# Weight-stationary blocks as three products of 256 columns into half a bank

## The chip, the core and the metric

The kernel runs on one core of a Trainium2 chip. The time is device microseconds (us) of one execution; lower is better. TensorE (PE) multiplies and has a second row in the profile for its weight loads (PEld); VectorE (DVE), ScalarE (ACT) and GpSimd (POOL) do the rest; SyncE (SP) issues the weight transfers. PSUM has eight banks of 512 fp32 columns on 128 partitions; the kernel uses four as accumulators (`acc`) and four for everything else (`aux`).

## The reference

One decoder block for 256 tokens and a model width of 2048, all in fp32:

```
a = rmsnorm(x) ; proj = a @ w_in            # 17408 columns
q_a, k_a, v_a, q_r, f_r, i_r, g_r, gate_a, gate_r = split(proj)
q, k = rotary(q_a), rotary(k_a)              # 3 groups x 8 heads of 128
A = windowed attention in 3 groups, mixed by their softmax denominators
R = gated linear recurrence (q_r, f_r, i_r), normed per head, times silu(g_r)
y = sigmoid(gate_a) * (A @ w_attn_branch) + sigmoid(gate_r) * (R @ w_hgrn_branch)
h = x + rmsnorm(y @ w_mix_out)
h = h + rmsnorm((silu(g) * u) @ w_ffn_down)  # g, u = rmsnorm(h) @ w_ffn_gate_up
```

## The kernel before

Every large product is made of fp32r matmuls. Each operand is split into a high part (rounded to fp32r by ACT, line L242 for weights) and a low part (the remainder, DVE, L243), and a product is high x high + high x low + low x high. The activations lie transposed in `xT` (`Split`): per `k` (128 of the 2048 inner rows) a slot holds the high part of 256 tokens and right behind it the low part, so the two can be read as 512 columns in a row; the third value that a call of `Split` returns, `both`, is that.

The work is a list of blocks, each cut into chunks of 512 KB of weights, and one loop runs over all chunks. In each turn it splits the weights of the chunk two ahead (ACT, then DVE), issues the load of the chunk eight ahead (SP), multiplies the present chunk, and then advances by one step each the oldest evacuation (`evacs`) and two lanes of side work (the two recurrences and the attention heads). Each is a Python generator, so what it issues stands in the engines' queues at that place. Engines take their queues in order. Waits come from the tiles' dependencies. There are two kinds of block:

- "N": activations stationary, weights moving. A block is 512 output columns; token half `s` has a bank of its own. Per `k` and half three matmuls of 512 columns. In the V blocks (`parity`) the stationary slice takes every second token.
- "W": weights stationary, activations moving, so that the result comes out transposed (heads on partitions). A block is 256 output columns, two heads, `s` = 0 and 1; 16 `k` in four chunks of four. There are 32 W blocks: for `f_r` and `q_r` (2 x 2 each) and for rotary `q` and `k` (24).

In a W block before, each head has a bank. Per `k` and head two matmuls: the high weights by `both` (512 columns, so the left half of the bank collects high x high and the right half high x low), and the low weights by the high activations (256 columns, added into the left half). The order of the two alternates with `k`. When the block is done, `both_halves` makes the sum: ACT copies the right halves to a tile `sum` (L200), DVE adds the left halves (L202), and the evacuation proper (`evac_f`, `evac_qr` or `evac_rope`) works from `sum` in SBUF. `evac_rope` does nothing in its first step, in its second multiplies the swapped halves by the sine table (L677, two operations on 64 partitions), and in its third multiplies `src` in place by the cosine table (L683) and adds the two into `qk` in an order with even tokens first (L684).

All matmuls pass through the helper at L115, the weight loads of W and N blocks alike. The recurrences' small products stand in PE's queue between the chunks; they wait for DVE's product L776, which follows the masked copy L787; POOL works for them at L770 and L777.

Of the kernel before, what the change touches and what calls it, by code (L numbers as in the profile page):

```python
# [16 lines left out]
AF = mybir.ActivationFunctionType  # L17
OP = mybir.AluOpType

P = 128  # L20
S = 256
# [56 lines left out]
def tile_hybrid_block(ctx: ExitStack, tc: tile.TileContext, t, out):  # L78
    nc = tc.nc
# [25 lines left out]
    def acc_bank():  # L105
        return accp.tile([P, 512], F32, tag="acc", name=nm("acc"))
# [7 lines left out]
    def mm(ps, lhsT, rhs, start, stop):  # L114
        nc.tensor.matmul(ps, lhsT, rhs, start=start, stop=stop, skip_group_check=True)  # L115
# [51 lines left out]
    def ptile(s):  # L167
        pool, n = (act_pool[0], 2) if act_pool else (fp, 5)
        return pool.tile([P, 512], F32, tag="p", bufs=n, name=nm(s))
# [16 lines left out]
    def add(*args, **kw):  # L186
        b = Block(*args, **kw)
        blocks.append(b)
        for c in range(b.steps):
            chunks.append([b, c, None, None, None])  # L190

    def add_wide(w, nk, col, xs, ev):
        for i in range(2):
            add("W", w, nk, col + 256 * i, xs, both_halves(ev, i))

    def both_halves(ev, i):
        def go(banks):
            s = ptile("sum").rearrange("p (h t) -> p h t", h=2)
            for n, ps in enumerate(banks):
                nc.scalar.activation(s[:, n, :], ps[:, S:], AF.Copy)  # L200
            for n, ps in enumerate(banks):
                nc.vector.tensor_add(s[:, n, :], ps[:, :S], s[:, n, :])  # L202
            yield from ev(i, s)
        return go

    def parts(j):

# [37 lines left out]
    def multiply(j, sides=(0, 1)):  # L245
        b, c = chunks[j][:2]
        wh, wl = (w.rearrange("p (k c) -> p k c", k=b.per) for w in chunks[j][3:])
        if b.banks is None:
            b.banks = [acc_bank() for _ in range(2)]
        for s in sides:  # L250
            if s == 1 and c == 0 and b.mid:
                b.mid()
            for kk in range(b.per):
                k = b.per * c + kk
                first, last = k == 0, k == b.nk - 1
                xh, xl, both = b.xs(k)
                if b.kind == "N":
                    ps = b.banks[s]
                    if b.parity:
                        sh, sl = (  # L260
                            x.rearrange("p (j two) -> p two j", two=2)[:, s, :]
                            for x in (xh, xl)
                        )
                    else:
                        sh, sl = (x[:, s * P : (s + 1) * P] for x in (xh, xl))
                    mm(ps, sh, wh[:, kk, :], first, False)
                    mm(ps, sh, wl[:, kk, :], False, False)
                    mm(ps, sl, wh[:, kk, :], False, last)
                    continue
                h, l = (w[:, kk, s * P : (s + 1) * P] for w in (wh, wl))  # L270
                pair = [(b.banks[s], h, both), (b.banks[s][:, :S], l, xh)]
                for i, (ps, x, y) in enumerate(pair if k % 2 == 0 else pair[::-1]):
                    mm(ps, x, y, first and i == 0, last and i == 1)

    def add_wide_block(*args, **kw):
        b = Wide(*args, **kw)
# [52 lines left out]
    def multiply_wide(n, sides=(0, 1), groups=(0, 1)):  # L329
        b, i = steps[n][:2]  # L330
        m, by7 = b.order[i]
        parity = wides.index(b) % 2

        def bank(key, side):
            if key not in b.bank:
                b.bank[key] = acc_bank() if (parity == 0) == (side == 1) else aux()
            return b.bank[key]

        def prod(key, x, w, j, last=False):
            ps = bank(key, 0 if type(key) is tuple else 1)  # L340
            wh, wl = (v[:, j * 512 : (j + 1) * 512] for v in w)
            mm(ps, x[0], wh, key not in b.open, False)
            mm(ps, x[0], wl, False, False)
            mm(ps, x[1], wh, False, last)
            b.open.add(key)

        def act_of(s, k):
            return [x[:, s * P : (s + 1) * P] for x in b.xs(2 * m + k)[:2]]

        w = steps[n][3]  # L350
        if not by7:
            for s in sides:
                for g in groups:
                    for k in range(2):
                        prod((s, g), act_of(s, k), w, 2 * g + k, i == len(b.order) - 1 and k == 1)
            return
        t, d, sums = w[:2], w[2:], b.seven(m)
        last = i == b.last7
        prod((0, 1), act_of(0, 1), d, 2)
        prod((0, 0), sums(3), d, 0)  # L360
        prod("p1", act_of(0, 0), d, 1, last)
        prod("p6", sums(1), t, 2, last)
        prod("p5", sums(0), t, 1, last)
        prod("p7", sums(2), t, 0, last)
        prod((1, 1), act_of(1, 1), t, 3)
# [29 lines left out]
    class Split:  # L395
# [6 lines left out]

        def __call__(self, k):
            x = self.slots[k // 2]
            both = self.flat[k // 2][:, k % 2 * 512 : k % 2 * 512 + 512]
            return x[:, k % 2, 0, :], x[:, k % 2, 1, :], both

        def f32(self, k):
            return self(k)[0].bitcast(F32)
# [256 lines left out]
    def evac_rope(key, tab, then=None):  # L666

        cos = tabs[:, tab, :]
        sin = tabs[:, tab + 1, :]

        def ev(i, src):
            if i == 0:
                qkT[key] = fslot("qk").rearrange("p (h t) -> p h t", h=4)
            yield
            w = ptile("w").rearrange("p (h t) -> p h t", h=2)
            for o, n in ((0, 64), (64, 0)):
                nc.vector.tensor_mul(  # L677
                    w[o : o + 64], src[n : n + 64],
                    sin[n : n + 64, None, :].to_broadcast([64, 2, S]),
                )  # L680
            yield
            u = src
            nc.vector.tensor_mul(u, src, by_rows(cos, 2))  # L683
            nc.vector.tensor_add(  # L684
                qkT[key][:, 2 * i : 2 * i + 2, :].rearrange("p h (two j) -> p h two j", two=2),
                u.rearrange("p h (j two) -> p h two j", two=2),
                w.rearrange("p h (j two) -> p h two j", two=2),
            )
            if i == 1 and then:
                then()  # L690
        return ev
# [5 lines left out]
    def attention(half, h):  # L697
        o = None
        for par in range(2):
            own = slice(par * P, (par + 1) * P)  # L700
            ps = aux()
            for g in range(3):
                q, k = qkT["q", half, g], qkT["k", half, g]
                if g == 0:
                    mm(ps[:, :S], q[:, h, own], k[:, h, :], True, True)
                else:
                    mm(ps[:, P * (g + 1) : P * (g + 2)], q[:, h, own], k[:, h, own], True, True)
            yield
            p = ptile("p")
            m = small("m")  # L710
            nc.vector.tensor_tensor_reduce(
                out=p, in0=ps, in1=amask[:, par, :], scale=1.0, scalar=3e38,
                op0=OP.add, op1=OP.min, accum_out=m[:, 0:1],
            )
            nc.scalar.activation(p, p, AF.Exp, scale=-1.0, bias=m[:, 0:1], accum_out=m[:, 1:2])
            yield
            nc.vector.reciprocal(m[:, 2:3], m[:, 1:2])
            nc.vector.tensor_scalar(p, p, m[:, 2:3], None, op0=OP.mult)
            yield
            yield  # L720
            ps = aux()
            for c in range(4):
                cols = slice(c * P, (c + 1) * P)
                nc.tensor.transpose(ps[:, cols], p[:, cols], ident)  # L724
            yield
            pt = ptile("pt")
            nc.scalar.activation(pt, ps, AF.Copy)
            yield
            if o is None:
                o = aux()  # L730
            for c in range(4):
                v = vN[half, max(c - 1, 0)][:, c if c < 2 else par, h * P : (h + 1) * P]
                mm(o[:, own], v, pt[:, c * P : (c + 1) * P], c == 0, c == 3)
            yield
        hi, lo, _ = attnT(4 * half + h)
        ov = o[:, :S].rearrange("p (two j) -> p two j", two=2)
        nc.scalar.activation(hi.rearrange("p (j two) -> p two j", two=2), ov, AF.Copy)
        nc.vector.tensor_sub(
            lo.rearrange("p (j two) -> p two j", two=2), ov,
            attnT.f32(4 * half + h).rearrange("p (j two) -> p two j", two=2),  # L740
        )
        yield
# [697 lines left out]
```

## Time and profile before

| what | value |
|---|---|
| time, median of 3 runs | 1741.58 us (1741.17 to 1743.07) |
| profiled execution | span 1740.1 us from its first to its last instruction (its only time on the page) |
| PE | 1725.0 us busy, 8424 matmuls, as many loads |
| DVE / ACT / POOL | 1264.3 / 886.1 / 74.0 us busy |
| DMA | 325.91 MB, mean 187 GB/s |
| W blocks | from 56 to 652 us of the span, with V, I and N work between |
| matmuls in W blocks | 1024 of 512 columns and 1024 of 256 |
| `sum`: L200 / L202 | 64 operations each, 20.5 us on ACT, 23.9 us on DVE |

A matmul's busy time in such a table runs from its start to a modelled end and overlaps the next one's; the distance from one start to the next is what counts for a stream of them. The groups of instructions name output and inputs as out<-in: `acc<-xT,w` are the W blocks' products, `acc<-w,xT` the N blocks'. A timeline row gives start, length, engine, line and the number of instructions merged into it. The idle time behind the bar of a group, with what ended it, is time in which that engine waited.

### The profile page before, as it was taken

How to read it: one execution, taken by the hardware profiler on the slowest of the kernel's cores; microseconds unless marked ns; L12 is line 12 of the kernel's file. 1: busy time of each engine (PE TensorE's matmuls, PEld its weight loads, DVE VectorE, ACT ScalarE, POOL GpSimd, SP SyncE). 2: the span in 40 equal slices, each digit the busy share in tenths (PEclk: the TensorE clock that was granted, in tenths of full speed). 3: DMA queues.
4: the chain of work that ended last, by engine and by line, in shares of the span. 5: the costliest groups of instructions: out<-in, count | busy, mean ns of one | idle time of the engine just before them, and what ended most of it. 6: DMA issues, size and time to landing. Idle time of an engine off the chain costs nothing.

```text
span 1740.1 us, 21588 instructions
## 1 busy us (share of the span) xinstructions
PE 1725.0 (99%) x8424; PEld 1448.6 (83%) x8424; DVE 1264.3 (73%) x1372; ACT 886.1 (51%) x1050; POOL 74.0 (4%) x54
## 2 busy tenths in 40 slices
PE   9999999999999999999999999999999999999997
PEld 7888888888888888888888877888888888888886
DVE  5767647877546776544566577888888888898998
ACT  6545455344444444454444466555555555665663
POOL 0002413400000000000000000000000000000000
PEclk9999999999999999999999999999999999999999
DMA  7655445455454554455555745655555555666553
GB/s 271 202 192 194 145 150 165 146 160 186 163 170 161 185 188 169 170 169 193 193 179 185 266 168 175 214 199 201 205 194 194 194 194 199 221 209 218 195 197 116
DMA packets 201222, 325.91 MB, mean 187 GB/s; under 512 B 10096, under 2 KB 76832, under 8 KB 201120
## 3 DMA queue, kind: packets, MB, share of 16 engines
q1 hardware_dynamic: 198848, 319.41, 54.4%
q10 hardware_dynamic: 2272, 5.12, 0.8%
q8 instruction: 66, 1.08, 0.2%
q14 instruction: 36, 0.29, 0.1%
HBM read 322.40 MB, written 2.10 MB: 186 GB/s over the span
## 4 chain that ended last, share of the span: by engine, by line
PE 95%; DVE 2%; ACT 1%; issue 1%; DMA 0%; POOL 0%; DVEq 0%; ACTq 0%
PE acc L115 71%; PE aux L115 22%; DVE w L243 1%; ACT w L242 1%; DVE w L677 0%; PE aux L453 0%; PE aux L724 0%; DMA gpost<-in_norm_mix_post 0%; PE acc L1127 0%; DVE fz L1256 0%; PE aux L1127 0%; DVE x L776 0%; PE aux L440 0%; ACT junk L1210 0%; POOL x L770 0%
## 5 line engine op out<-in xcount | busy, mean ns | idle before, releaser
L243 DVE TENSOR_TENSOR w<-raw,w 128x1024 fp32r<-128x1024 f32 (+1 forms) x353 | 444.4, 1260 | 365.5 <-ACT w L242 362.7
L242 ACT ACTIVATE w<-raw 128x1024 fp32r<-128x1024 f32 (+1 forms) x353 | 372.9, 1057 | 481.1 <-PE acc L115 470.7
L115 PE MATMUL acc<-w,xT 128*128 128x512 f32 x1728 | 409.1, 395 | 0.0
L115 PEld LDWEIGHTS acc<-w,xT 128*128 128x128 f32 x1728 | 326.3, 191 | 65.8
L115 PE MATMUL acc<-xT,w 128*128 128x256 f32 (+1 forms) x2048 | 362.6, 338 | 0.0
L115 PEld LDWEIGHTS acc<-xT,w 128*128 128x128 f32 x2048 | 313.0, 189 | 45.1
L308 DVE TENSOR_TENSOR wl<-raw,w 128x2048 fp32r<-128x2048 f32 x82 | 187.5, 2287 | 34.0 <-ACT w L306 33.9
L306 ACT ACTIVATE w<-raw 128x2048 fp32r<-128x2048 f32 x82 | 156.6, 1910 | 81.7 <-PE aux L115 32.1
L115 PE MATMUL acc<-w,hT 128*128 128x512 f32 x622 | 182.5, 392 | 1.5 <-DVE w L243 1.2
L115 PEld LDWEIGHTS acc<-w,hT 128*128 128x128 f32 x622 | 115.8, 188 | 26.9 <-DVE w L243 2.5
L115 PE MATMUL aux<-w,hT 128*128 128x512 f32 x430 | 135.7, 389 | 0.0
L324 DVE TENSOR_TENSOR wl<-sum,w 128x2048 fp32r<-128x2048 f32 x42 | 96.2, 2290 | 33.8 <-ACT w L320 32.7
L317 ACT ACTIVATE w<-sum 128x1024 fp32r<-128x1024 f32 x42 | 44.7, 1063 | 111.0 <-DVE sum L312 106.7
L115 PEld LDWEIGHTS aux<-w,hT 128*128 128x128 f32 x430 | 80.7, 188 | 16.7
L115 PE MATMUL acc<-w,yT 128*128 128x512 f32 x384 | 88.0, 390 | 0.3 <-DVE w L243 0.3
L115 PEld LDWEIGHTS acc<-w,yT 128*128 128x128 f32 x384 | 71.8, 188 | 15.5 <-DVE w L243 0.7
L115 PE MATMUL acc<-w,a 128*128 128x512 f32 x268 | 83.7, 389 | 0.0
L115 PE MATMUL aux<-w,a 128*128 128x512 f32 x268 | 83.7, 389 | 0.0
L115 PE MATMUL aux<-wl,hT 128*128 128x512 f32 x215 | 83.7, 389 | 0.0
L115 PE MATMUL acc<-wl,hT 128*128 128x512 f32 x215 | 83.7, 389 | 0.0
L326 DVE TENSOR_TENSOR dl<-raw,dh 128x1536 fp32r<-128x1536 f32 x42 | 73.5, 1751 | 0.0
L323 ACT ACTIVATE dh<-raw 128x1536 fp32r<-128x1536 f32 x42 | 61.9, 1474 | 0.0
(263 smaller groups left out, 2015.3 us busy)
## 6 DMA issues: line engine op xcount, KB each, us to landing
raw<-in_w_in SPq DMA_DIRECT2D x271, 512.0 KB, 4.5
raw<-in_w_ffn_gate_up SPq DMA_DIRECT2D x176, 512.0 KB, 4.4
raw<-in_w_ffn_down SPq DMA_DIRECT2D x88, 512.0 KB, 4.8
raw<-in_w_mix_out SPq DMA_DIRECT2D x32, 512.0 KB, 4.9
raw<-in_w_attn_branch SPq DMA_DIRECT2D x16, 512.0 KB, 4.5
raw<-in_w_hgrn_branch SPq DMA_DIRECT2D x16, 512.0 KB, 4.6
hx<-in_x ACTq DMA_DIRECT2D x4, 512.0 KB, 9.9
x<-in_x SPq DMA_DIRECT2D x3, 512.0 KB, 10.0
```

Source lines behind the costliest of these rows:

```text
L115: nc.tensor.matmul(ps, lhsT, rhs, start=start, stop=stop, skip_group_check=True)
L242: nc.scalar.activation(wh[:, k], raw[:, k], AF.Copy)
L243: nc.vector.tensor_sub(wl[:, k], raw[:, k], wh[:, k].bitcast(F32))
L306: nc.scalar.activation(hi, raw, AF.Copy)
L308: nc.vector.tensor_sub(lo, raw, hi.bitcast(F32))
L317: nc.scalar.activation(hi[:, :1024], s[:, :1024], AF.Copy)
L323: nc.scalar.activation(dhi, d, AF.Copy)
L324: nc.vector.tensor_sub(lo, s, hi.bitcast(F32))
L326: nc.vector.tensor_sub(dlo, d, dhi.bitcast(F32))
```

## The change

A W block uses one bank: head `s` = 0 the left half, `s` = 1 the right. Per `k` and head there are three matmuls of 256 columns into that half: high weights by high activations, high weights by low activations, low weights by high activations. The high weights are loaded for each of the two. Only the block's very first matmul carries the start flag, since it resets the whole bank. The sum is thus complete in the bank: `both_halves` with its copies and additions is gone, and the evacuations are handed the bank itself. As the bank is not overwritten in place, `evac_rope` now writes the cosine product, already in the even-first order, into `qk` and adds the sine product there. `both` goes away.

```diff
-            add("W", w, nk, col + 256 * i, xs, both_halves(ev, i))
-
-    def both_halves(ev, i):
-        def go(banks):
-            s = ptile("sum").rearrange("p (h t) -> p h t", h=2)
-            for n, ps in enumerate(banks):
-                nc.scalar.activation(s[:, n, :], ps[:, S:], AF.Copy)
-            for n, ps in enumerate(banks):
-                nc.vector.tensor_add(s[:, n, :], ps[:, :S], s[:, n, :])
-            yield from ev(i, s)
-        return go
+            add("W", w, nk, col + 256 * i, xs, both_heads(ev, i))
+
+    def both_heads(ev, i):
+        return lambda banks: ev(i, banks[0].rearrange("p (h t) -> p h t", h=2))
...
-            b.banks = [acc_bank() for _ in range(2)]
+            b.banks = [acc_bank() for _ in range(2 if b.kind == "N" else 1)]
...
-                xh, xl, both = b.xs(k)
+                xh, xl = b.xs(k)
...
                 h, l = (w[:, kk, s * P : (s + 1) * P] for w in (wh, wl))
-                pair = [(b.banks[s], h, both), (b.banks[s][:, :S], l, xh)]
-                for i, (ps, x, y) in enumerate(pair if k % 2 == 0 else pair[::-1]):
-                    mm(ps, x, y, first and i == 0, last and i == 1)
+                ps = b.banks[0][:, s * S : (s + 1) * S]
+                mm(ps, h, xh, first and s == 0, False)
+                mm(ps, h, xl, False, False)
+                mm(ps, l, xh, False, last)
...
-            u = src
-            nc.vector.tensor_mul(u, src, by_rows(cos, 2))
-            nc.vector.tensor_add(
-                qkT[key][:, 2 * i : 2 * i + 2, :].rearrange("p h (two j) -> p h two j", two=2),
-                u.rearrange("p h (j two) -> p h two j", two=2),
-                w.rearrange("p h (j two) -> p h two j", two=2),
-            )
+            d = qkT[key][:, 2 * i : 2 * i + 2, :].rearrange("p h (two j) -> p h two j", two=2)
+            nc.vector.tensor_mul(
+                d,
+                src.rearrange("p h (j two) -> p h two j", two=2),
+                cos.rearrange("p (j two) -> p two j", two=2)[:, None, :, :]
+                .to_broadcast([P, 2, 2, P]),
+            )
+            nc.vector.tensor_add(d, d, w.rearrange("p h (j two) -> p h two j", two=2))
```

More of the change, by code (lines that the diff above doesn't have):

```diff
@@ L347, in act_of @@
         def act_of(s, k):
-            return [x[:, s * P : (s + 1) * P] for x in b.xs(2 * m + k)[:2]]
+            return [x[:, s * P : (s + 1) * P] for x in b.xs(2 * m + k)]
         w = steps[n][3]
@@ L404, in __call__ @@
             x = self.slots[k // 2]
-            both = self.flat[k // 2][:, k % 2 * 512 : k % 2 * 512 + 512]
-            return x[:, k % 2, 0, :], x[:, k % 2, 1, :], both
+            return x[:, k % 2, 0, :], x[:, k % 2, 1, :]
         def f32(self, k):
@@ L734, in attention @@
             yield
-        hi, lo, _ = attnT(4 * half + h)
+        hi, lo = attnT(4 * half + h)
         ov = o[:, :S].rearrange("p (two j) -> p two j", two=2)
```

## The prediction

> **What bounds the kernel now.** I read the page first: totals, chain, groups.
>
> ```profile
> span 1740.1 us, 21588 instructions
> PE 1725.0 (99%) x8424; PEld 1448.6 (83%) x8424; DVE 1264.3 (73%) x1372; ACT 886.1 (51%) x1050; POOL 74.0 (4%) x54
> PE 95%; DVE 2%; ACT 1%; issue 1%; DMA 0%; POOL 0%; DVEq 0%; ACTq 0%
> L115 PE MATMUL acc<-xT,w 128*128 128x512 f32 x1024 | 327.3, 398 | 0.0
> L115 PE MATMUL acc<-xT,w 128*128 128x256 f32 x1024 | 201.8, 278 | 0.0
> ```
>
> TensorE is busy for 99% of the span and carries 95% of the chain. The last two rows (groups with shapes kept apart) are the products that the change touches: 1024 of 512 columns and 1024 of 256, stationary `w`, moving `xT`. I call one of each, the work of one `k` and one side, a pair. There are 1024 pairs. A matmul's duration overlaps the next one's, so the mean of 398 ns is no price; the spacing of starts is. For that I took the chain of waits in a stretch that holds only such blocks, and then the timeline of PE in long even stretches.
>
> ```profile
> 559.91 80.12 PE acc L115 x460
> 545.81 94.45 PE L115 MATMUL acc<-xT,w 128*128 128x512 f32 x541
> 764.62 77.68 PE L115 MATMUL acc<-w,xT 128*128 128x512 f32 x342
> 433.69 6.70 PE L115 MATMUL acc<-w,xT 128*128 128x512 f32 x28
> L115 PE MATMUL acc<-w,xT 128*128 128x512 f32 x355 | 80.6, 389 | 0.0
> L115 PE MATMUL acc<-w,xT 128*128 128x512 f32 x28 | 6.7, 394 | 0.0
> ```
>
> The first row is the whole chain from 560 to 640 us: PE alone. So in these blocks a nanosecond per pair is a nanosecond of the kernel, and all other work is cover. Second row (start, length, count): leaving off the last matmul's 0.40 us (398 ns above), 540 spacings fill 94.05 us, 174.2 ns each, **348.3 ns a pair**. Third row: an "N" block (512-column products only, stationary `xT`): (77.68 - 0.39) / 341 = 226.7 ns. Fourth row: the same in a V block, whose stationary slices take every second element: (6.70 - 0.39) / 27 = 233.6 ns. The 0.39 is the mean duration in the last two rows, the groups of 760 to 840 and of 434 to 440 us.
>
> **The change on PE.** A pair (512 and 256 columns, two weight loads) becomes a triple (three times 256 columns, three weight loads). Columns stay at 768; one matmul with its load is added, 1024 times. The one question is what a matmul costs beyond its columns.
>
> Take a matmul as a + c for 256 columns. The N block says a + 2c = 226.7, the pair 2a + 3c = 348.3; so c = 2 x 226.7 - 348.3 = 105.1 and a = 16.5 ns. That is the upper end: +16.5 ns a triple. For the lower end I need the fastest that 512 columns go past anywhere:
>
> ```profile
> 1022.26 1.47 PE L115 MATMUL aux<-warm 128*128 128x512 bf16 x6
> 1023.57 0.27 PE L453 MATMUL aux<-ident,h 128*128 128x128 f32 x1
> 208.72 1.90 PE L115 MATMUL aux<-ones,x 128*128 128x1 f32 x16
> L115 PE MATMUL aux<-ones,x 128*128 128x1 f32 x32 | 3.8, 249 | 0.0
> ```
>
> Six 512-column matmuls on `warm` occupy 1023.57 - 1022.26 = 1.31 us, 218 ns each, anything fixed included. 768 columns at that rate are 327 ns, so the pair holds at least (348.3 - 327) / 2 = 10.6 ns beyond columns per matmul. Third row: matmuls with one moving column and a fresh 128-column load each come every (1.90 - 0.25) / 15 = 110 ns, so a load alone fills about 110 ns and just fits behind 256 columns.
>
> Why should a hidden load cost anything? The V blocks show it: only the layout of the stationary operand differs, and every 512-column matmul takes 6.9 ns more (233.6 against 226.7), though a load of 110 ns has 226 to hide in. So loading is not free for the stream beside it. I take the middle of 10.6 and 16.5, 13.6 ns: the lower end counts what is fixed in a `warm` matmul as columns, so it is too low, and the upper one holds only if a column of moving `xT` costs what a column of moving `w` does, which no row shows. 1024 x 13.6 ns = **+13.9 us** (bounds +10.9 and +16.9).
>
> The Trainium skill ("TensorE: Matmul & The Clock Gate", part 2, on LDWEIGHTS) says the opposite: PE has two independent read ports, and loading the next weights takes no bandwidth from the running matmul. Its section on the back-to-back issue gap would make the addition about 2.5 ns, an estimate of 1024 x 2.5 ns = 2.6 us. The V blocks' 6.9 ns disagree, so the sum does not go by it.
>
> **The change beside PE.** Rows from the groups with shapes kept apart:
>
> ```profile
> L200 ACT ACTIVATE sum<-acc 128x256 f32<-128x256 f32 x64 | 20.5, 371 | 0.0
> L202 DVE TENSOR_TENSOR sum<-acc,sum 128x256 f32<-128x256 f32 x64 | 23.9, 415 | 0.0
> L677 DVE TENSOR_TENSOR w<-sum,tabs 64x512 f32<-64x512 f32 x48 | 39.4, 820 | 1.1
> L683 DVE TENSOR_TENSOR sum<-sum,tabs 128x512 f32<-128x512 f32 x24 | 16.4, 684 | 0.0
> L684 DVE TENSOR_TENSOR qk<-sum,w 128x512 f32<-128x512 f32 x24 | 16.6, 692 | 1.0
> L1015 DVE TENSOR_TENSOR zg<-acc,gpost 128x512 f32<-128x512 f32 x8 | 5.5, 683 | 4.4 <-DMA gpost<-in_norm_mix_post 4.4
> ```
>
> - Removed: 64 ACT copies (20.5 us) and 64 DVE additions (23.9 us). In the even blocks the chain is PE alone, so this returns nothing there. If they had been on the path it would be 44 us.
> - L677, L683 and the products with `rowb` read the bank instead of `sum`. L1015 reads a bank at 683 ns, L683 reads `sum` at 684: no difference. The stride of two moves from the add into the product as well; L684 already reads both inputs with that stride at 692 ns. At worst 8 ns on 24 operations, hidden.
> - The bank is now held until the product at L683 has read it, in the third step after the block, about three chunks. A chunk is 8 pairs, 2.8 us, so 8.4 us. Against that a block takes one bank of four instead of two, so a bank comes up again four blocks (44 us) later; where a V block follows and takes two, the older block ended 11 us before. Cost nothing; without that cover PE would wait up to 8.4 us at such a place. Waits of DVE on PE do not move ahead: the split of the next chunk stands before the evacuation in DVE's queue, as now.
> - No DMA and nothing in SP's or POOL's queue is moved. Weight chunks are consumed more slowly, so loads and splits get easier.
>
> **Where DVE does stop PE.** Only beside the second recurrence (waits of PE, timelines of POOL and DVE, line L787, L677 from 560 to 640 us, stretches):
>
> ```profile
> PE aux L115 <- DVE x L776: 2.0, 3, 1.5
> 295.32 1.27 POOL L777 TENSOR_TENSOR x<-x,q 128x512 f32<-128x512 f32 x1 [1.91 <-ACT x L774]
> 296.56 2.47 POOL L770 TENSOR_TENSOR x<-b 128x1024 f32<-128x1024 f32 x1
> 295.43 4.15 DVE L677 TENSOR_TENSOR w<-sum,tabs 64x512 f32<-64x512 f32 x2
> 302.07 1.31 DVE L787 COPY_PREDICATED at<-lmask,aux 128x512 f32<-128x512 int32 x1
> L787 DVE COPY_PREDICATED at<-lmask,aux x12: 702/725/1320, 173.7 to 333.8; 128x512 f32<-128x512 int32 x12
> L677 DVE TENSOR_TENSOR w<-sum,tabs 64x512 f32<-64x512 f32 x14 | 9.6, 685 | 0.3
> 303.00:307.00 4.00, 2.55 (x21) 2.35 (x21) 4.00 (x3) 1.60 (x3) 3.32 (x2) 0.99 0.00 0
> 307.00:310.00 3.00, 3.00 (x12) 2.51 (x11) 3.00 (x6) 0.00 (x0) 0.00 (x0) 0.50 0.46 131
> ```
>
> PE loses 2.0 us in three waits on L776, 1.45 of it between 303 and 307 (busy 2.55 of 4.00), and right after it the granted clock is 0.50, 3 us that give back half, 1.5 us. Before that wait two L677 take 4.15 us while POOL works instead of 2 x 0.685. After the change L677 has one operand less in SBUF, and PE comes later by 4% in the same stretch. Both shrink the wait: at most all of it and the slow clock, -3.5 us; at worst another slow stretch, +1.5. I take -2.0. Here a page speaks too: the Trainium skill ("SBUF — State Buffer", who interferes with whom) has only DVE operations with two SBUF inputs contend with POOL's reads, which would take L677 out of it. L787 reads one of its inputs from a bank and still took 1.31 us under POOL against a median of 0.725, so I count on about half.
>
> **Sum.** The executions' median (1741.58) lies 1.5 us over this execution's span; I add to the median: 1741.6 + 13.9 - 2.0 = **1753.5 us**, +0.7%. Its own range: 1741.6 + 10.9 - 3.5 = 1749 to 1741.6 + 16.9 + 1.5 = 1760.
>
> **The rivals.** *Spacings as recorded (faster).* Single starts in an even stretch:
>
> ```profile
> 100.31 0.39 PE L115 MATMUL acc<-xT,w 128*128 128x256 f32 x2
> 100.43 0.51 PE L115 MATMUL acc<-xT,w 128*128 128x256 f32 x2
> 100.54 0.40 PE L115 MATMUL acc<-xT,w 128*128 128x512 f32 x1
> 100.77 0.39 PE L115 MATMUL acc<-xT,w 128*128 128x512 f32 x1
> ```
>
> The starts of a 256-column matmul and its successor lie 0.12 and 0.11 us apart, 0.115 on average, those of a 512-column one 0.23. If 115 ns is what such a matmul costs in any company, the triple takes 345 ns, 3.3 less than the pair: -3.4 us, with -2.0 at DVE's waits 1736 us. It decides if a matmul of 256 columns can keep under 116.1 ns (a third of 348.3) in a row of its own kind. For it: it is the operation itself. Against: it makes the 512-column matmul 233, while N blocks with the same shapes do it in 226.7, and nothing explains that; if instead the short ones run ahead and the long ones pay, the pair comes out by the N blocks' rate. Only sums over a whole period are safe.
>
> *Same columns, same time.* If the pair's 348.3 is a rate per column and loads are hidden, the triple takes 348.3 too: 1741.6 - 2.0 = 1739.6, no change. This is what the skill's two ports would give. Against it stand the V blocks again.
>
> *Loads become the bound (slower still).* 110 ns of load behind 109 of columns leaves no slack. If the load stretches by what it takes from the stream, 110 + 16.5 = 126.5 ns, a triple takes 379.5, +31.2 ns, +31.9 us: 1772 us. Against: two short matmuls in a row show no such spacing now.
>
> **How the numbers follow.** Chances: fixed cost per matmul 0.64 (1753.5), recorded spacings 0.18 (1736), same time 0.11 (1739.6), loads bound 0.07 (1772). 0.2% (3.5 us) is about what a measurement of this kernel can tell from no change. The first and last are slower: 0.71. Recorded spacings are faster: 0.18. Same: 0.11. The range goes from 1736, which takes in the case of no change and the upper half of the faster one, to 1761, just above the likeliest one's own end; left out are half of the faster case (0.09) and the loads as the bound (0.07).
>
> **What would show it.** In the changed kernel a long even stretch of 256-column products on `xT` gives the spacing directly: 120.6 ns if I am right (a third of 348.3 + 13.6; 119.6 to 121.6 by the bounds), 115 or 116 for the rivals, 126 if loads bind. PE's matmuls rise by 1024 to 9448. L200 and L202 are gone; products reading the bank stay near 684 ns; L677's two under POOL are shorter, the wait on L776 below 2.0 us and the clock near 307 us whole. N blocks stay at 226.7 and V blocks at 233.6 ns. I am wrong if the triple is under 352 ns, or if PE begins to wait for a bank at the start of a block.

## Result and profile after

| | before | after |
|---|---|---|
| median, 4 runs each | 1741.55 us (1741.17 to 1743.07) | 1749.51 us (1746.70 to 1750.67) |
| ratio | | 1.0043, 95% interval 1.0028 to 1.0057 |
| profiled execution: time, span | span 1740.1 us | 1750.67 us, span 1748.9 us |

The change costs 8.0 us. 1753.5 was forecast, in a range of 1736 to 1761. Page of the changed kernel:

```profile
span 1748.9 us, 23501 instructions
PE 1735.6 (99%) x9447; PEld 1505.7 (86%) x9448; DVE 1238.7 (71%) x1308; ACT 868.6 (50%) x986; POOL 73.1 (4%) x54
L115 PE MATMUL acc<-xT,w 128*128 128x256 f32 x3072 | 374.1, 284 | 0.0
L115 PEld LDWEIGHTS acc<-xT,w 128*128 128x128 f32 x3072 | 371.3, 193 | 0.3
```

PE has its 1024 matmuls more (one record is missing), DVE and ACT have lost 64 operations each, and the loads of the W blocks now fill practically the whole of their stretches (371.3 us beside 374.1). A load's record lasts 193 ns and starts come every 120, so the records overlap; a full row does not yet say that loads are the limit. The timeline of PE in even stretches, columns start, length, ..., count; the last row is the group of 560 to 640 us, with the mean duration:

```profile
559.73 95.44 PE L115 MATMUL acc<-xT,w 128*128 128x256 f32 x794
774.74 75.64 PE L115 MATMUL acc<-w,xT 128*128 128x512 f32 x333
438.73 7.62 PE L115 MATMUL acc<-w,xT 128*128 128x512 f32 x32
L115 PE MATMUL acc<-xT,w 128*128 128x256 f32 x669 | 80.4, 283 | 0.0
```

(95.44 - 0.28) / 793 = **120.0 ns** a product, 360.0 ns a triple against 348.3 ns a pair: 11.7 ns, and 1024 of them are 12.0 us. The N block (75.25 / 332 = 226.7 ns) and the V block (7.23 / 31 = 233 ns) stand where they stood. So 4.0 us of the 12.0 came back elsewhere. The waits of PE, then DVE and POOL beside the second recurrence, then two windows (the last three columns are granted clock, DMA share and GB/s):

```profile
PE aux L115 <- DVE x L770: 0.3, 1, 0.3
298.98 1.39 DVE L670 TENSOR_TENSOR w<-acc,tabs 64x512 f32<-64x512 f32 x2
304.46 1.34 DVE L781 COPY_PREDICATED at<-lmask,aux 128x512 f32<-128x512 int32 x1
298.88 1.28 POOL L771 TENSOR_TENSOR x<-x,q 128x512 f32<-128x512 f32 x1 [2.10 <-ACT x L768]
300.12 2.02 POOL L764 TENSOR_TENSOR x<-b 128x1024 f32<-128x1024 f32 x1
306.42 2.16 POOL L771 TENSOR_TENSOR x<-x,q 128x512 f32<-128x512 f32 x1 [4.28 <-ACT x L768]
306.00:310.00 4.00, 4.00 (x37) 4.00 (x36) 3.31 (x4) 1.33 (x2) 3.58 (x2) 1.00 0.32 93
334.00:337.30 3.30, 3.30 (x17) 3.30 (x17) 1.30 (x1) 0.00 (x0) 0.00 (x0) 0.50 0.00 0
```

L770 is the old L776: PE waits for it 0.3 us instead of 2.0. L670 is the old L677: two of them take 1.39 us under POOL, where they took 4.15 before. The clock is whole between 306 and 310 (1.00), but a slow stretch of about 3.4 us now stands at 334 to 337 (0.50).

### The profile page after: what moved, and what is told of

Same layout as the page of the kernel before. It is cut to its first block, busy times and chain, and to the rows that moved or that the text cites. A ratio compares the mean times of both kernels' runs of the same rounds, so it can differ in the third digit from the quotient of the medians.

```text
span 1748.9 us, 23501 instructions
## 1 busy us (share of the span) xinstructions
PE 1735.6 (99%) x9447; PEld 1505.7 (86%) x9448; DVE 1238.7 (71%) x1308; ACT 868.6 (50%) x986; POOL 73.1 (4%) x54
## 4 chain that ended last, share of the span: by engine, by line
PE 96%; DVE 1%; ACT 1%; DMA 1%; issue 1%; POOL 0%; SPq 0%; DVEq 0%; ACTq 0%
PE acc L115 72%; PE aux L115 22%; ACT w L235 0%; DMA raw<-in_w_in 0%; PE aux L718 0%; DMA gpost<-in_norm_mix_post 0%; DVE w L236 0%; PE aux L446 0%; PE acc L1121 0%; DVE fz L1250 0%; PE aux L1121 0%; PE aux L433 0%; ACT junk L1204 0%; POOL x L764 0%; DVE e L1200 0%
## 5 line engine op out<-in xcount | busy, mean ns | idle before, releaser
L115 PE MATMUL acc<-xT,w 128*128 128x256 f32 x3072 | 374.1, 284 | 0.0
L115 PEld LDWEIGHTS acc<-xT,w 128*128 128x128 f32 x3072 | 371.3, 193 | 0.3
```

## Experiments

Each spacing below is the PE timeline's length less the last product's duration (0.28 us for 256 columns, 0.39 to 0.40 for 512), divided by the count less one. Times with an interval are medians against runs of the kernel before on the same chip; those without are one run.

**The two halves of the change.** First the products alone, with the old evacuation:

```diff
-                pair = [(b.banks[s], h, both), (b.banks[s][:, :S], l, xh)]
-                ...
+                left, right = b.banks[s][:, :S], b.banks[s][:, S:]
+                mm(left, h, xh, first, False)
+                mm(right, h, xl, False, last)
+                mm(left, l, xh, False, last)
```

> The three products of 256 columns alone; two banks per block, the copies and additions of before stay. The change added 11.7 ns to each of 1024 pairs (348.3 to 360.0 ns in even stretches), 12.0 us, and the time rose by only 8.0. Theory A: the products cost the full 12 us and the lighter evacuation gives 4 us back, in the stretch of the second recurrence. Then this kernel takes 1741.5 + 12.0 = 1753.5 us, at most 1 us less since later products shorten DVE's waits. Theory B: the evacuation gives nothing back and the products cost 8 us, because waits swallow the rest: 1749.5 us. Triples at 360.0 ns in either case.

Then the evacuation alone, on top of the changed kernel:

```diff
-                mm(ps, h, xh, first and s == 0, False)
-                mm(ps, h, xl, False, False)
-                mm(ps, l, xh, False, last)
+                pair = [(b.banks[0], h, both), (half, l, xh)]
+                ...
```

> The evacuation alone: products of 512 and 256 columns as before, but all into one bank, which the evacuations read directly, without copies and additions. It leaves out keeping the two heads apart (their sums run together in the bank), so only its time counts. Theory A: 1741.5 - 4 = 1737.5 us (between 1736 and 1739), with PE's waits on the product of line L776's kind gone beside the second recurrence. Theory B: 1741.5 us. Pairs at 348.3 ns in even stretches in either case.

Measured: products alone 1752.21 us against 1741.33, ratio 1.0060 (1.0046 to 1.0073); evacuation alone 1737.53 against 1741.33, ratio 0.9980 (0.9971 to 0.9989). Waits of PE, products alone and then evacuation alone:

```profile
PE aux L115 <- DVE x L777: 1.7, 2, 1.4
```

```profile
PE aux L115 <- DVE x L771: 0.3, 1, 0.3
```

+10.9 and -3.8 us make +7.1; both together gave +8.0. Theory A stands, by the second run: the interval of the first (+8.0 to +12.7 us) still touches theory B's 8, but B gave the evacuation nothing, and in the second run even the upper end of the interval (0.9989) is below 1. The wait beside the recurrence goes with the evacuation, not with the products. What made the wait stands in the chain of work from 280 to 330 us, before and then with the evacuation alone:

```profile
by line: PE acc L115 42.5%; DVE w L677 16.4%; PE aux L115 13.9%; DVE w L243 9.8%; ACT w L242 4.3%; DVE at L787 4.1%; DVE x L776 3.4%; issue 3.3%; DVE sum L683 2.4%; DVE qk L684 0.2%; DVEq L243 0.1%
by line: PE acc L115 76.1%; PE aux L115 24.7%; issue 0.0%
```

Before, the chain runs through the slow L677; the copies and additions (L200, L202) are not on it. Afterwards it is PE alone. By this it was the sine product's read from the bank that shortened the chain, rather than the 44 us of work that went away; no run has the one without the other.

The shares of the two halves are clearer without the clock. Executions differ in how many stretches at half clock they hold, 3.41 us each, which cost 1.7: the profiles of before, after and the evacuation alone hold two in the W blocks' stretch, that of the products alone none. First and last start of a W product, in the order before, products alone, evacuation alone, after:

```profile
L115 PE MATMUL acc<-xT,w x2048: 273/392/629, 56.2 to 651.5; 128*128 128x512 f32 x94, 128*128 128x256 f32 x93
L115 PE MATMUL acc<-xT,w x3072: 278/283/385, 56.2 to 659.5; 128*128 128x256 f32 x192
L115 PE MATMUL acc<-xT,w x2048: 273/392/628, 56.0 to 649.0; 128*128 128x512 f32 x94, 128*128 128x256 f32 x93
L115 PE MATMUL acc<-xT,w x3072: 278/283/415, 56.6 to 661.0; 128*128 128x256 f32 x192
```

595.3 us before, 593.0 with the evacuation alone, 604.4 after, each with two such stretches: the evacuation gives 2.3 us, 1.7 of it by the wait, and the whole change costs 9.1. The products alone took 603.3 without any; taking 3.4 us off before's 595.3, they cost 11.4. The medians of the evacuation fit: executions with a mean granted clock of 0.997 took 1738.0 us with it (8 of them) and 1740.3 before (9), again 2.3. The rest of its 3.8 us is the clock: 0.9973 on average against 0.9964, 1.6 us of 1740. Whether the light evacuation brings the better clock is not shown.

**What a product costs beyond its columns.** The changed kernel gives the two numbers that the prediction lacked: a + c = 120.0 and, from N blocks, a + 2c = 226.7. So 256 columns take c = 106.7 ns and a = 13.3 ns. By that a pair would take 2a + 3c = 346.7; it took 348.3. I changed the order within the pairs of the kernel before:

```diff
-                for i, (ps, x, y) in enumerate(pair if k % 2 == 0 else pair[::-1]):
-                    mm(ps, x, y, first and i == 0, last and i == 1)
+                mm(b.banks[s], h, both, first, False)
+                mm(b.banks[s][:, :S], l, xh, False, last)
```

> Before, with the two products of a pair always in the order 512, 256 instead of alternating. Theory 1 (each weight load takes 13.3 ns from the stream, whatever its neighbours): a pair takes 768 columns and two loads, 320.0 + 26.7 = 346.7 ns if 512 columns are 226.7 - 13.3 = 213.4 ns; 1.6 ns less than the alternating pair at most, so 346.7 to 348.3 ns and 1739.9 to 1741.5 us. Rival (a 256-column product costs 115 ns and a 512-column one 233 by themselves): 348.3 ns and each start where its size puts it, 115 after a 256 and 233 after a 512.

```profile
555.72 94.46 PE L115 MATMUL acc<-xT,w 128*128 128x512 f32 x544
63.66 72.59 PE L115 MATMUL acc<-xT,w 128*128 128x512 f32 x410
```

From 556 us on a pair takes about 347 ns, as the two equations say. But from 64 us it takes about 353, in the same code, and the whole was 1743.5 us, ratio 1.0012 (1.0003 to 1.0020). Neither theory had that. In this order two even rhythms were seen, and the alternating order's 348.3 stands between them; what chooses is not known. Long rows of 256-column products showed one rhythm only (120.0 ns). One assumption is left in the 13.3 ns: that a column of moving `xT` (first equation) takes as long as one of moving `w` (second).

**Is it the load?** Stationary slices with a stride of two, in the changed kernel:

```diff
-                h, l = (w[:, kk, s * P : (s + 1) * P] for w in (wh, wl))
+                h, l = (w[:, kk, s::2] for w in (wh, wl))
```

> The changed kernel with stationary slices that take every second element of the 256, as the V blocks do with xT. It computes other columns' places (heads mixed), only its time counts. Theory 1 (the load takes time from the stream, by its layout): the 6.9 ns that a V block's 512-column matmul takes more, on each 256-column matmul too: 126.9 ns instead of 120.0, 3072 x 6.9 = 21.2 us, 1771 us. Theory 2 (a fixed cost for each fp32r matmul, and something else in V blocks): 120.0 ns and 1749.5 us. Theory 3 (120 ns is the period of the loads, which bound): V's loads show 193 to 194 ns instead of 188, so 125 to 126 ns, 1766 us.

```profile
63.72 72.52 PE L115 MATMUL acc<-xT,w 128*128 128x256 f32 x603
```

72.24 / 602 = 120.0 ns, 1750.8 us (ratio 1.0055, 1.0037 to 1.0074). The layout alone does nothing here; theory 1, in the form in which I had put it, fell. Next, the V blocks themselves, contiguous, in the kernel before:

```diff
-                    if b.parity:
+                    if False:
```

> The kernel before with the V blocks' stationary slices contiguous instead of every second token (their values then stand at other tokens' places, so only its time counts). The stride of two left 256-column products at 120.0 ns where weights are stationary. Theory L (the stride costs a 512-column matmul 6.9 ns): V blocks at 226.7 ns instead of 233.6, 576 x 6.9 = 4.0 us, 1737.4 us. Theory M (the 6.9 ns belong to the place in the program, not to the layout): 233.6 ns and 1741.4 us.

```profile
428.25 8.12 PE L115 MATMUL acc<-w,xT 128*128 128x512 f32 x35
```

7.73 / 34 = 227 ns: the stride was what V blocks paid for. 1736.64 us against 1741.58, ratio 0.9975 (0.9965 to 0.9984). The same stride in the kernel before's pairs:

```diff
-                h, l = (w[:, kk, s * P : (s + 1) * P] for w in (wh, wl))
+                h, l = (w[:, kk, s::2] for w in (wh, wl))
```

> The kernel before, its pairs of 512 and 256 columns with stationary slices of every second element of the 256 (heads mixed, only the time counts). With 256-column products only, the same slices cost nothing (120.0 ns); in V blocks with 512 columns they cost 6.9 ns. Theory P: the stride costs a 512-column product 6.9 ns wherever it stands, so a pair takes 348.3 + 6.9 = 355.2 ns and the kernel 1748.6 us. Theory Q: it costs only when the strided operand is xT, so 348.3 ns and 1741.5 us.

```profile
63.80 72.37 PE L115 MATMUL acc<-xT,w 128*128 128x512 f32 x410
```

About 352 ns a pair, 1742.8 us: half of what P expected. This run does not decide: another order alone, without a stride, put pairs at 347 or 353 ns, so the 352 can be the stride's price or another rhythm. What stands is that the stride costs 6.9 ns in rows of 512-column products and nothing in rows of 256; how it is paid stays open. The number of stationary columns, at one layout:

```diff
+                if k:
+                    ps, h, l = ps[:64], h[:, :64], l[:, :64]
```

> The changed kernel with stationary tiles of 64 columns instead of 128 for all but the first inner slice of each block (the other half of each head is left out of the sums). Half the load, the same moving columns. Theory 2 (fixed cost) 120.0 ns a product still, 1749.5 us. Theory 1 (the load takes 13.3 ns from the stream, in proportion to its columns): 113.3 ns, 2880 x 6.7 = 19 us less, 1730 us. Theory 3 (the load's period is what shows): a load of half the columns is done in about 60 ns, so the 106.7 to 109 ns of the columns are left, 30 to 38 us less, 1712 to 1720 us.

```profile
63.73 72.50 PE L115 MATMUL acc<-xT,w 128*64 128x256 f32 x635
```

72.22 / 634 = 113.9 ns, with one product in sixteen still at full width, so 113.5 for the narrow ones; 1730.94 us where 1730 was expected. Half the stationary columns, half of the 13.3 ns: 120.0 - 113.5 = 6.5. Twice that, 13.0 ns, is a found from W products alone, if the cost goes with the stationary columns. A fixed cost per product is out, and a load that merely binds (106.7 to 109) too. Not separated: with 64 columns the product also uses half of the array's columns, so "the load" and "the array columns" go together here.

**Where do loads bind?** Products of 128 columns, and a stride of four:

```diff
+                for n in range(2):
+                    ps = b.banks[0][:, s * S + n * P : s * S + (n + 1) * P]
+                    yh, yl = (x[:, n * P : (n + 1) * P] for x in (xh, xl))
+                    ...
```

> The changed kernel with each 256-column product cut into two of 128 columns: 6144 products, loads doubled, columns the same. Theory 2 (a fixed 13.3 ns for each fp32r matmul beside its columns, loads hidden): 53.3 + 13.3 = 66.7 ns each, 133.3 ns for two, 3072 x 13.3 = 41 us more, 1790 us. Theory 3 (a load has a period of its own, and 120.0 ns is that period): 120 ns each, 240 for two, 3072 x 120 = 369 us more, 2118 us. In between: 110 ns, the spacing of one-column products with a load each in the kernel before; then loads bind here at 110, 2057 us, and the 120.0 of 256 columns is not a load's period.

```diff
-                h, l = (w[:, kk, s * P : (s + 1) * P] for w in (wh, wl))
+                h, l = (
+                    w.rearrange("p (s c f) -> p s f c", s=2, f=4)[:, s, kk, :]
+                    for w in (chunks[j][3], chunks[j][4])
+                )
```

> The changed kernel with stationary slices of every fourth element (heads mixed, only the time counts). Every second element left a 256-column product at 120.0 ns. If a load takes from the stream only by its number of columns: 120.0 ns and 1749.5 us. If a wider stride makes each load longer, its period rises above 120 ns and binds: a load of twice the 111 ns of a one-column product's spacing would give 222 ns and 1749.5 + 313 = 2063 us.

```profile
63.73 72.52 PE L115 MATMUL acc<-xT,w 128*128 128x128 f32 x648
```

```profile
63.66 72.73 PE L115 MATMUL acc<-xT,w 128*128 128x256 f32 x311
```

128 columns: 72.24 / 647 = 111.7 ns, 2105.7 us (3072 x 103.4 ns would be 318 us more than the changed kernel; it is 356, and the mean granted clock of this execution was 0.978 instead of 0.997, about 40 us). That 111.7 ns is the load's own period shows in the kernel before, in rows of small products of 64 moving columns with 128 and with 64 stationary ones:

```profile
206.99 1.89 PE L115 MATMUL aux<-x 128*128 128x64 f32 x16
223.41 1.15 PE L115 MATMUL aux<-x 128*64 128x64 f32 x16
```

With mean durations of 0.27 and 0.23 us they come every 108 and 61 ns: the moving columns hardly matter, the stationary ones do. The load's period is under 120, so at 256 columns the stream with its 13.3 ns is the limit, by 8 ns. Stride four: (72.73 - 0.39) / 310 = 233.4 ns (a product's record lasts 0.39 us in this run), 2097.7 us. The spacing is twice the load's period above, so the load has become about twice as long and binds.

**A version from it.** Pairs, with triples and the light evacuation only in the six W blocks beside the recurrence, and contiguous slices in the first group's V blocks (`parity=g > 0`, natural key order in scores and mask):

> A version that uses what the runs showed: pairs as before, but three products into one bank and the light evacuation in the six W blocks (8 to 13) beside the second recurrence, where the changed kernel took 87.7 us against 88.1; and the two V blocks of the first group with contiguous slices (their keys in natural order in scores and mask). Sum: -0.4 us in those six blocks by the profiles (as much as -1.7 if the evacuation is worth 4 us there and six blocks of triples cost 2.3), -192 x 6.9 ns = -1.3 us if the stride is what costs V blocks. 1738.4 to 1739.7 us; 1739.7 to 1741 if it is not.

1739.9 us against 1741.58, ratio 0.9993 (0.9984 to 1.0002). It cannot be told from the kernel before. Contiguous slices in all V blocks would be worth more (e8), but the second and third group need their keys by parity.

## Why the prediction was right

- *PE is the path in even stretches, so a nanosecond per triple counts 1024 times.* Right: 12.0 us by spacings, 10.9 by medians for the products alone, 11.4 in their profile without the clock.
- *One more matmul costs 13.6 ns (10.6 to 16.5).* 120.0 ns a product lies in the 119.6 to 121.6 that it implied. As a difference to the pair it was 11.7, so this term of the sum was 1.9 us too large. The two equations took the pair for 2a + 3c; it holds 1.6 ns more than that, and part of it was booked to a. That the middle of the two bounds, 6 ns apart, came within 0.3 ns of a's 13.3 is luck; the interval was earned, the point in it was not.
- *V blocks show that loads are not free.* The conclusion holds, by the 64-column run; the reason given was weak. The stride does cost V blocks their 6.9 ns, but costs 256-column products nothing, so it was no measure of what a load takes.
- *The LDWEIGHTS rule of the Trainium skill ("TensorE: Matmul & The Clock Gate", part 2): loading takes no read bandwidth from the running matmul.* No run here measures the bandwidth, but for these fp32r products a load is not free: 6.5 ns less with half the stationary columns (and half of the array's columns in use).
- *Evacuation and bank.* Right: L676, the cosine product from the bank, takes 683 ns where L683 took 684, and L670 688; PE waits for no bank.

```profile
L670 DVE TENSOR_TENSOR w<-acc,tabs 64x512 f32<-64x512 f32 x48 | 33.0, 688 | 1.1
L676 DVE TENSOR_TENSOR qk<-acc,tabs 128x512 f32<-128x512 f32 x24 | 16.4, 683 | 0.0
```

- *DVE's waits give back 2.0 us.* They gave 2.3 at the same granted clock, 3.8 by medians; the term counted waits and clock together (-3.5 to +1.5), so by medians it was too small by half, and its lower end was just passed. I had halved the effect since L787 took 1.31 us under POOL with an input in a bank. That was a misreading: L781, the same line, takes 1.34 us at 304.46 while POOL is idle from 302.14 to 306.42. The rule of the Trainium skill ("SBUF — State Buffer", who interferes with whom), that a TENSOR_TENSOR of DVE contends with GpSimd's reads when both of its inputs are in SBUF, agrees with L670, which has one input in a bank (1.39 us for two under POOL, 4.15 before with both in SBUF). What else slows L781 is not shown.
- *A slow clock near 307 goes.* There, yes; another came at 334, so no gain from it shows in this profile: both hold two such stretches in the W blocks. Nor do the runs tie the slow clock to the wait: the products alone waited 1.7 us in their profile and held no such stretch, the evacuation alone waited 0.3 us and held two.
- The faster rival (115 ns) fell with 120.0 in a long row: single starts in a mixed sequence are no price. So did "same columns, same time" and "loads become the bound", the last by only 8 ns.

By spacings and medians the two errors (1.9 us too much, 2 us too little given back) have the same sign: 1753.5 instead of 1749.5. At the same granted clock, where the change costs 9.1 us instead of 8.0, nearly all of what is left is the price of the products (11.4 instead of 13.9).

## What to carry to other kernels

Count matmuls, not only columns: here each fp32r product with 128 stationary columns cost about 13 ns beside its columns, so two products of 512 and 256 beat three of 256 (348.3 against 360.0 ns) even though the three need no addition afterwards. Take a price from the sum over a long even stretch, best of one shape. Before a difference of a few us is booked to a change, compare executions of the same granted clock. And an elementwise operation that is hidden on average can still be worth feeding from PSUM where it runs beside GpSimd and stands on the chain: L677 did (4.15 against 1.39 us).

## What was not expected of the hardware

- Products of 512 and 256 columns in a fixed order ran at about 347 or 353 ns a pair in different stretches of one execution.
- A stationary stride of two costs 6.9 ns a product in rows of 512 columns and nothing in rows of 256; a stride of four makes the load the bound at 233.4 ns.
- The granted clock drops to 0.50 for 3.4 us while PE shows no idle time (334 to 337 us). With 128-column products it was 0.55 on average from 456 to 541 us, PE again busy throughout.
